# A two-block transformer forward pass: the opening of block 1 with four parts' modulation columns on TensorE, rotation tables made earlier, and more buffers for whole weights

## The chip, the cores and the metric

The kernel runs on one core of a Trainium2 chip. One launch computes everything. The metric is device microseconds of that launch; before the change it is 1609.81 us, the median of three runs (1606.74 to 1617.44).

The engines are named as the profile names them: PE is TensorE (PEld is its weight loading), DVE is VectorE, ACT is ScalarE, POOL is GpSimd, SP is the engine whose queue issues the loads.

## What is computed

256 tokens of 1024 features pass through two transformer blocks. Block 1 has block attention, a recurrent mixer (RWKV7) and an expert layer; block 2 has two attentions and a gated layer. What matters here is how block 1 begins:

```python
def first_block(x, c, positions, w_ada, b_ada, norm1_g, w_in, ...):
    mod = (jax.nn.silu(c) @ w_ada[l] + b_ada[l])[:, None, :]
    sh1, sc1, gt1, sh2, sc2, gt2 = jnp.split(mod, 6, axis=-1)
    xn = rms_norm(h, norm1_g[l]) * (1.0 + sc1) + sh1
    proj = xn @ w_in[l]
    qm, km, vm, zrw, gate_logits = jnp.split(proj, split_at, axis=-1)
    qm = rope_partial(rms_norm(qm ...), positions)
    ...
    zrw = token_shift(zrw, rwkv_mu[l])
    zr, zk, zv, zw, za, zg = jnp.split(zrw, rwkv_split, axis=-1)
    ...
```

`c` is one vector of 1024 numbers, so `mod` is a vector; `sh1` and `sc1` are its first 2048 entries (shift and scale). `rms_norm` divides each token by the root of the mean of its squares. `rope_partial` multiplies by the sine and cosine of positions times frequencies.

## The kernel before, in words

**Layout.** Activations stand transposed, 128 features on the partitions and 256 tokens along the free axis, in eight chunks. All weights come from HBM as units of 128 x 1024 float32 (512 KB), loaded by SP's queue in an order that is written out. Most matmuls are made of three passes: a weight unit `raw` is split by ACT into `hi` (line 304, a rounded copy) and by DVE into `lo = raw - hi` (line 306), the activations are split likewise into `xh` and `xl`, and PE sums `xh` by `hi`, `xl` by `hi` and `xh` by `lo`.

**The opening.** `block1_mixer` opens with the first norm, its modulation and the first products, woven together over eight parts `d` of 128 features. Ahead of the loop, eight `sq` tiles (`x` squared, line 660) are summed over the partitions by matmuls with a matrix of ones into `ss` (line 661). The loop of line 705 then runs `n` from 0 to 9 and calls three functions, each one step behind the last:

- `open_ada(n)` loads two units `aw` of `w_ada` (line 668). Each holds four 128 x 256 blocks; the 256 columns are 128 of shift and 128 of scale for part `n`. DVE multiplies each block with a column of `silu(c)`, held in the tile `sil`, and adds it up in `aacc`, 128 x 256: one pass on line 672 and seven on line 674. For every second part it also loads a unit `whole` (line 678), and for each part a unit that is split into `hi` and `lo`.
- `open_norm(n - 1)` sums `aacc` over the partitions by two matmuls with one column of ones (line 687), which gives shift and scale as two 128 x 1 columns in PSUM. DVE adds `b_ada` (line 689, `mod`) and makes the gain column `gs` (line 431). `norm_chunk` then makes the normalized tile: `nt` on DVE (line 437, `x` times gain times `rs`, the inverse root that `norm_stat` made of `ss` on lines 368 and 369), `xh` on ACT (438), `x` on ACT (440, the unsplit tile), `xl` on DVE (441).
- `open_mm(n - 2)` multiplies part `n - 2` into six PSUM tiles `z` of 128 x 512: eight matmuls of `xh` by `hi`, four of `x` by `whole` in float32 (line 703), eight of `xl` by `hi`, eight of `xh` by `lo` (line 699).

At `n == 1`, ahead of the three calls, stand `rope_tables` (the load of `pos`, eleven DVE passes, and sine and cosine on ACT, lines 592 to 611), the load of ACT's table for logarithm and exponential (it shows at line 708), and `norm_stat`. Sine needs another ACT table, which is loaded at line 607.

**What sets the order.** A scheduling layer puts the instructions in a fixed order for each engine; an engine works through its own list and waits by semaphores for the others. Pools of buffers set when a load may be issued: `aw` has 5 buffers, `whole` 2, `aacc` 3, `x` 3, `hi` and `lo` 4 each in the opening, `raw` 4, and the small PSUM tiles `mmo` 2.

After the opening, the same `z` tiles are shifted by one token and the rest of both blocks follows.

Of the kernel before, what the change touches and what calls it, by code (L numbers as in the profile page):

```python
# [6 lines left out]
F32 = mybir.dt.float32  # L7
# [9 lines left out]
T = 256  # L17
# [15 lines left out]
W3 = 1  # L33
NS = 2
AHEAD = 1
DECAY = float(np.exp(-0.5))

AT_B1, AT_U, AT_V, AT_B2, AT_FF = 192, 192, 192, 192, 192
# [231 lines left out]
class Prog:  # L270
# [360 lines left out]
    def block1_mixer(self):  # L631
        tc, v, s, pe, sy = self.tc, self.v, self.s, self.pe, self.sy
        wu, bp, mm = self.wu, self.bp, self.pe.matmul
# [9 lines left out]
        def shift(ps, mi, dst):  # L643
            s.activation(dst, ps, AF.Copy, scale=omm[:, mi:mi + 1])
            v.scalar_tensor_tensor(dst[:, 1:], ps[:, :T - 1], self.col("mu", mi), dst[:, 1:], OP.mult, OP.add)


        with ExitStack() as st:
            E = st.enter_context
            sp = E(tc.tile_pool(name="open", bufs=1, side="right", reuse_waits="tile"))  # L650
            zp = E(tc.tile_pool(name="zps", bufs=1, space=PSUM, reuse_waits="tile"))
            h = sp.tile([128, 8, T], F32, name="x0")
            for q in range(2):
                sy.dma_start(h[:, 4 * q:4 * q + 4], self.a["xT"][:, 4 * q:4 * q + 4])
            zps = [zp.tile([128, 2, T], F32, name=f"z{j}") for j in range(6)]
            slabs, whole, xs = [], [], {}
            ss = self.mm.tile([128, T], F32, name="mmo", tag="mm")
            for d in range(8):
                sq = sp.tile([128, T], F32, name="sq", tag="sq", bufs=6)
                s.activation(sq, h[:, d], AF.Square)  # L660
                mm(ss, self.ones, sq, start=(d == 0), stop=(d == 7))
            accs = {}

            def open_ada(d):
                accs[d] = acc = sp.tile([128, T], F32, name="aacc", tag="aacc", bufs=3)
                for i in range(2):
                    w = sp.tile([128, 4, T], F32, name="aw", tag="aw", bufs=5)
                    sy.dma_start(w, self.a["w"][wu["ada0"] + 2 * d + i].rearrange("p (k n) -> p k n", k=4))
                    for k in range(4):
                        sc = self.silu["c"][:, 4 * i + k:4 * i + k + 1]  # L670
                        if i + k == 0:
                            v.tensor_scalar(acc, w[:, k], sc, None, OP.mult)
                        else:
                            v.scalar_tensor_tensor(acc, w[:, k], sc, acc, OP.mult, OP.add)
                u = wu["rw"] + d // 2 * 3
                if d % 2 == 0:
                    whole.append(sp.tile([128, 1024], F32, name="whole", tag="whole", bufs=2))
                    sy.dma_start(whole[-1], self.a["w"][u])
                slabs.append(self.wsplit(u + 1 + d % 2, pool=sp, bufs=4, lead=0))
                if d == 3:  # L680
                    sy.dma_start(self.c0, self.a["w"][wu["c0"]])

            def open_norm(d):
                acc = accs.pop(d)
                pm = self.mm.tile([128, 2], F32, name="mmo", tag="mm")
                for i in range(2):
                    mm(pm[:, i:i + 1], acc[:, i * 128:(i + 1) * 128], self.ones[:, 0:1], start=(i == 0), stop=(i == 1), skip_group_check=True)
                for i in range(2):
                    v.tensor_tensor(self.mod1[:, 8 * i + d:8 * i + d + 1], pm[:, i:i + 1], self.col("b1", 8 * i + d), OP.add)
                gs = self.norm_gain("n1", self.mod1[:, 8 + d:9 + d], 1, d)  # L690
                xs[d] = sp.tile([128, T], F32, name="x", tag="x", bufs=3)
                self.norm_chunk(h[:, d], gs, self.mod1[:, d:d + 1], xh[:, d], xl[:, d], xs[d])

            def open_mm(d):
                hi, lo = slabs[d]
                C = lambda i: slice(i * 128, (i + 1) * 128)
                for part, (lhs, rhs) in enumerate(((hi, xh), (hi, xl), (lo, xh))):
                    for j in range(4, 12):
                        mm(zps[j // 2][:, j % 2], lhs[:, C(j - 4)], rhs[:, d], start=(d + part == 0 and j % 2 == 0),
                           stop=(d == 7 and part == 2), skip_group_check=True)  # L700
                    if part == 0:
                        for j in range(4):
                            mm(zps[j // 2][:, j % 2], whole[d // 2][:, C(d % 2 * 4 + j)], xs[d], start=(d + j % 2 == 0), stop=(d == 7), skip_group_check=True)

            for n in range(10):
                if n == 1:
                    self.rope_tables()
                    tc.keep_in_program_order(s.preload_act_table_set(LN_EXP))
                    self.norm_stat(ss)
                for f, d in ((open_ada, n), (open_norm, n - 1), (open_mm, n - 2)):  # L710
                    if 0 <= d < 8:
                        f(d)
            zs = []

            def shift_z(c):
                for i in range(3):
                    z = e4("z")
                    j = 3 * c + i
                    shift(zps[j // 2][:, j % 2], (4, 0, 8)[i] + c, z)
                    zs.append(z)  # L720

            zwa, sg = bp.tile([128, T], F32, name="zwa"), bp.tile([128, T], F32, name="sg")
            thw = bp.tile([128, T], F32, name="thw")
            v.memset(thw[64:128], 0.0)
            shift_z(0)
            shift(self.t_unit(wu["rwl"], xh, xl), 12, zwa)
            t0 = self.sm.tile([128, T], F32, name="t0", tag="nt", bufs=2)
            s.activation(t0[0:64], zwa[0:64], AF.Exp, scale=-2.0)
            v.tensor_scalar(t0[0:64], t0[0:64], 2.0 ** 60, None, OP.min)
            s.activation(t0[0:64], t0[0:64], AF.Ln, bias=1.0)  # L730
            s.activation(t0[0:64], t0[0:64], AF.Exp, scale=-1.0)
            v.tensor_scalar(thw[0:64], t0[0:64], 2.0, -1.0, OP.mult, OP.add)
            v.memset(zwa[0:64], 0.0)
            shift_z(1)
            shift(self.t_unit(wu["rwl"] + 1, xh, xl), 13, sg)
            t0 = self.sm.tile([128, T], F32, name="t0", tag="nt", bufs=2)
            self.sigmoid(sg, sg, t0)
            shift_z(2)
            shift_z(3)
# [25 lines left out]
        def rwkv_pair(c):  # L765
# [6 lines left out]
            self.sigmoid(ld, ps, t0, nw0[:, c:c + 1])  # L772
            s.activation(ld, ld, AF.Copy, scale=-DECAY)
            L = e1("L")
# [234 lines left out]
        def fill():  # L1009
            yield from self.tn_steps(wu["mv"], 4, xh, xl, [vm[:, 0], vm[:, 1]], pp, "gm")  # L1010
            yield from staggered([moba_pair(c) for c in range(4)], 3)
            for j in range(16):
                ps = self.t_unit(wu["gate"] + j, xh, xl)
                t0 = e1("t0", "eg", 2)
                gt = e4("gt")
                self.sigmoid(gt, ps, t0)
                self.gates.append(gt)
                yield
            for j in range(4):
                for i, ps in enumerate(self.t_units(*self.wsplit(wu["pmr"] + 2 * j), 4, 2, mh, ml, 1024, [(pp, "gm")])):  # L1020
                    g = self.gates[4 * j + 2 * i]
                    v.tensor_tensor(g, ps, g, OP.mult)
                yield

        f, n, tick = fill(), 0.0, 0
# [41 lines left out]
    def peer(self):  # L1067
# [230 lines left out]
        while i < 128:  # L1298
            for _ in u_pair(i):
                n += 1  # L1300
                new = []
                while prog["c"] < T and prog["c"] // 4 * (left - AHEAD) <= n * (T // 4):
                    new.append(choose(gp))
# [484 lines left out]
```

## Time and profile before

| | before |
|---|---|
| median of three runs | 1609.81 us (1606.74 to 1617.44) |
| the profiled execution | 1610.28 us |
| its span in the trace | 1608.0 us, 33360 instructions |
| PE busy | 1562.9 us (97%) |
| PEld busy | 1504.4 us (94%) |
| DVE busy | 1263.5 us (79%) |
| ACT busy | 1019.4 us (63%) |
| the opening, up to its last `z` matmul | 69.94 us |
| DMA, mean over the span | 189 GB/s |

The trace is of one execution. An engine's busy time counts its own instructions alone; what an engine waited for is inferred from semaphores. "Idle before" is the time in which the engine had nothing to do ahead of that instruction, with what ended it. PEclk is the share of full clock that TensorE was granted: 1.00 is 2.4 GHz, 0.50 is 1.2 GHz. In the timeline, instructions of one line that follow each other are one row with a count; a row's time includes the latency of its last instruction, so a row may overlap the next of its engine. A float32 matmul leaves two records, the others leave one.

### The profile page before, as it was taken

The numbers are of one execution on the slowest core, as the hardware profiler recorded it, in microseconds if no ns is written. First come the engines' busy times: TensorE is split into PE (matmuls) and PEld (weight loads), VectorE is DVE, ScalarE is ACT, GpSimd is POOL, SyncE is SP. The second block draws the span as 40 slices with busy tenths as digits, with TensorE's granted clock in tenths as the row PEclk, the third lists the DMA queues.
The fourth block names the chain that finished last, engine by engine and source line by source line (L and its number), as shares of the span: only waits on it lengthen the run. The fifth ranks groups of instructions, "written<-read, shape, count | busy, mean of one in ns | idle before, by whom it ended". The sixth has DMA issues, their size and how long they took to land.

```text
span 1608.0 us, 33360 instructions
## 1 busy us (share of the span) xinstructions
PE 1562.9 (97%) x13022; PEld 1504.4 (94%) x13022; DVE 1263.5 (79%) x2731; ACT 1019.4 (63%) x2093; POOL 6.5 (0%) x43
## 2 busy tenths in 40 slices
PE   5999999999999999999999999999999999999998
PEld 5888898989999999999999999999888998989998
DVE  7887887878789777888877777777798986777776
ACT  4475765555545799998654445444679786665553
POOL 0000000000000000000000000000000000000000
PEclk8999999999999999999999999999999999999999
DMA  8632336645544544444688878788666322435553
GB/s 308 247 106 93 119 128 225 231 141 179 183 166 170 184 161 169 169 159 171 212 275 274 274 261 278 269 287 271 203 211 224 133 87 102 168 121 186 190 189 105
DMA packets 85261, 306.63 MB, mean 191 GB/s; under 512 B 9456, under 2 KB 10992, under 8 KB 84976
## 3 DMA queue, kind: packets, MB, share of 16 engines
q1 hardware_dynamic: 85104, 304.51, 55.4%
q8 instruction: 102, 1.67, 0.4%
q14 instruction: 55, 0.45, 0.1%
HBM read 303.42 MB, written 1.05 MB: 189 GB/s over the span
## 4 chain that ended last, share of the span: by engine, by line
PE 85%; DVE 8%; ACT 3%; DMA 2%; issue 1%; SPq 0%; DVEq 0%; ACTq 0%
PE mmo L322 14%; PE mmo L325 14%; PE mmo L323 14%; PE acc L322 7%; PE acc L323 7%; PE acc L325 7%; DVE lo L306 3%; DMA raw<-w 2%; PE pg L1263 2%; PE facc L322 1%; PE facc L325 1%; PE facc L323 1%; ACT hi L304 1%; PE pxt L893 1%; PE pz L881 1%
## 5 line engine op out<-in xcount | busy, mean ns | idle before, releaser
L304 ACT ACTIVATE hi<-raw 128x1024 fp32r<-128x1024 f32 (+1 forms) x465 | 490.4, 1057 | 370.0 <-PE mmo L323 136.1
L306 DVE TENSOR_TENSOR lo<-raw,hi 128x1024 fp32r<-128x1024 f32 (+1 forms) x465 | 565.2, 1218 | 165.7 <-ACT hi L304 162.6
L322 PE MATMUL mmo<-xh,hi 128*128 128x256 f32 x2032 | 498.8, 286 | 1.6 <-ACT hi L304 0.6
L323 PE MATMUL mmo<-xl,hi 128*128 128x256 f32 x2032 | 490.4, 281 | 0.0
L322 PEld LDWEIGHTS mmo<-xh,hi 128*128 128x128 f32 x2032 | 382.8, 189 | 5.7 <-ACT hi L304 2.1
L323 PEld LDWEIGHTS mmo<-xl,hi 128*128 128x128 f32 x2032 | 383.3, 189 | 1.9 <-issue 0.2
L325 PE MATMUL mmo<-xh,lo 128*128 128x256 f32 x2032 | 283.3, 281 | 4.7 <-DVE lo L306 4.6
L325 PEld LDWEIGHTS mmo<-xh,lo 128*128 128x128 f32 x2032 | 255.6, 189 | 7.2 <-DVE lo L306 6.5
L322 PE MATMUL acc<-Hh,hi 128*128 128x256 f32 x1024 | 241.8, 278 | 0.5 <-ACT Hh L363 0.5
L323 PE MATMUL acc<-Hl,hi 128*128 128x256 f32 x1024 | 241.0, 278 | 0.0
L322 PEld LDWEIGHTS acc<-Hh,hi 128*128 128x128 f32 x1024 | 192.3, 188 | 0.7 <-ACT Hh L363 0.7
L323 PEld LDWEIGHTS acc<-Hl,hi 128*128 128x128 f32 x1024 | 192.5, 188 | 0.1
L325 PE MATMUL acc<-Hh,lo 128*128 128x256 f32 x1024 | 139.4, 277 | 0.0
L325 PEld LDWEIGHTS acc<-Hh,lo 128*128 128x128 f32 x1024 | 127.3, 188 | 0.0
L388 DVE SCALAR_TENSOR_TENSOR acc<-raw,sil,acc 128x1024 f32<-128x1024 f32 x70 | 89.8, 1283 | 44.8 <-DMA raw<-w 44.7
L1245 ACT ACTIVATE D<-iota,i 128x128 f16<-128x128 f16 x256 | 84.6, 404 | 0.2
L1252 DVE TENSOR_TENSOR B<-O,iT 128x512 f16<-128x512 f16 x128 | 46.1, 417 | 0.0
L323 PE MATMUL facc<-Hl,hi 128*128 128x256 f32 x176 | 42.8, 281 | 0.0
L322 PE MATMUL facc<-Hh,hi 128*128 128x256 f32 x176 | 42.8, 281 | 0.0
L364 DVE TENSOR_TENSOR Hl<-hidA,Hh 128x256 fp32r<-128x256 f32 x96 | 40.0, 418 | 0.0
L363 ACT ACTIVATE Hh<-hidA 128x256 fp32r<-128x256 f32 x96 | 38.2, 400 | 0.0
L1246 ACT ACTIVATE A<-D 128x512 f16<-128x512 f16 x64 | 37.8, 628 | 0.0
(503 smaller groups left out, 2273.3 us busy)
## 6 DMA issues: line engine op xcount, KB each, us to landing
raw<-w SPq DMA_DIRECT2D x542, 512.0 KB, 4.1
aw<-w SPq DMA_DIRECT2D x16, 512.0 KB, 7.3
raw<-w SPq DMA_DIRECT2D x6, 384.0 KB, 3.3
whole<-w SPq DMA_DIRECT2D x4, 512.0 KB, 7.2
c<-w SPq DMA_DIRECT2D x3, 512.0 KB, 6.2
x<-xT SPq DMA_DIRECT2D x2, 512.0 KB, 5.7
hres<-xT SPq DMA_DIRECT2D x1, 1024.0 KB, 5.5
sk<-w SPq DMA_DIRECT2D x2, 512.0 KB, 5.6
```

The lines of the kernel that those rows point to most:

```text
L304: self.s.activation(hi[:, :n], r[:, :n], AF.Copy)
L306: self.v.tensor_tensor(lo[:, :n], r[:, :n], hi[:, :n].bitcast(F32), OP.subtract)
L322: m(out, whi[w], xhi[x], start=start, stop=False, skip_group_check=True)
L323: m(out, whi[w], xlo[x], start=False, stop=False, skip_group_check=True)
L325: m(out, wlo[w], xhi[x], start=False, stop=stop, skip_group_check=True)
L363: self.s.activation(hi, src, AF.Copy)
L364: self.v.tensor_tensor(lo, src, hi.bitcast(F32), OP.subtract)
L388: v.scalar_tensor_tensor(acc, w, sc, acc, OP.mult, OP.add)
L1245: s.activation(D[:, j], iota, AF.Abs, bias=i1[:, t0 + j:t0 + j + 1])
L1246: s.activation(A, D, AF.Relu, scale=-1.0, bias=1.0)
L1252: v.tensor_tensor(B[p], O, row(1 + p), OP.mult)
L1263: mm(pg[:, j], B[p][:, :, j], A[:, j], start=(j + p == 0), stop=(j == 3 and p == 1), skip_group_check=True)
```

## The change

Three edits, all in the opening.

1. For the parts `d < PEADA = 4`, `open_ada` makes no DVE passes. Instead, PE takes each 128 x 128 half of an `aw` block as its weights and the column of `silu(c)` as its one moving column: 2 units x 4 blocks x 2 halves are 16 float32 matmuls of one column for each part, 64 in all. They add up shift and scale in the small PSUM tile at once, so that for these parts `open_norm` needs no sums by ones and no `aacc`. Parts 4 to 7 are as before.
2. `rope_tables`, ACT's table loads and `norm_stat` stand at `n == 0` in place of `n == 1`, that is ahead of the first part's modulation.
3. `whole` has four buffers in place of two, and `sq` four in place of six.

```diff
--- before.py
+++ after.py
@@ -33,6 +33,7 @@
 W3 = 1
 NS = 2
 AHEAD = 1
+PEADA = 4
 DECAY = float(np.exp(-0.5))
 
 AT_B1, AT_U, AT_V, AT_B2, AT_FF = 192, 192, 192, 192, 192
@@ -656,25 +657,33 @@
             slabs, whole, xs = [], [], {}
             ss = self.mm.tile([128, T], F32, name="mmo", tag="mm")
             for d in range(8):
-                sq = sp.tile([128, T], F32, name="sq", tag="sq", bufs=6)
+                sq = sp.tile([128, T], F32, name="sq", tag="sq", bufs=4)
                 s.activation(sq, h[:, d], AF.Square)
                 mm(ss, self.ones, sq, start=(d == 0), stop=(d == 7))
             accs = {}
 
             def open_ada(d):
-                accs[d] = acc = sp.tile([128, T], F32, name="aacc", tag="aacc", bufs=3)
+
+                if d < PEADA:
+                    accs[d] = self.mm.tile([128, 2], F32, name="mmo", tag="mm")
+                else:
+                    accs[d] = acc = sp.tile([128, T], F32, name="aacc", tag="aacc", bufs=3)
                 for i in range(2):
                     w = sp.tile([128, 4, T], F32, name="aw", tag="aw", bufs=5)
                     sy.dma_start(w, self.a["w"][wu["ada0"] + 2 * d + i].rearrange("p (k n) -> p k n", k=4))
                     for k in range(4):
                         sc = self.silu["c"][:, 4 * i + k:4 * i + k + 1]
-                        if i + k == 0:
+                        if d < PEADA:
+                            for r in range(2):
+                                mm(accs[d][:, r:r + 1], w[:, k, r * 128:(r + 1) * 128], sc, start=(i + k + r == 0),
+                                   stop=(i == 1 and k == 3 and r == 1), skip_group_check=True)
+                        elif i + k == 0:
                             v.tensor_scalar(acc, w[:, k], sc, None, OP.mult)
                         else:
                             v.scalar_tensor_tensor(acc, w[:, k], sc, acc, OP.mult, OP.add)
                 u = wu["rw"] + d // 2 * 3
                 if d % 2 == 0:
-                    whole.append(sp.tile([128, 1024], F32, name="whole", tag="whole", bufs=2))
+                    whole.append(sp.tile([128, 1024], F32, name="whole", tag="whole", bufs=4))
                     sy.dma_start(whole[-1], self.a["w"][u])
                 slabs.append(self.wsplit(u + 1 + d % 2, pool=sp, bufs=4, lead=0))
                 if d == 3:
@@ -682,8 +691,8 @@
 
             def open_norm(d):
                 acc = accs.pop(d)
-                pm = self.mm.tile([128, 2], F32, name="mmo", tag="mm")
-                for i in range(2):
+                pm = acc if d < PEADA else self.mm.tile([128, 2], F32, name="mmo", tag="mm")
+                for i in range(2) if d >= PEADA else ():
                     mm(pm[:, i:i + 1], acc[:, i * 128:(i + 1) * 128], self.ones[:, 0:1], start=(i == 0), stop=(i == 1), skip_group_check=True)
                 for i in range(2):
                     v.tensor_tensor(self.mod1[:, 8 * i + d:8 * i + d + 1], pm[:, i:i + 1], self.col("b1", 8 * i + d), OP.add)
@@ -703,7 +712,7 @@
                             mm(zps[j // 2][:, j % 2], whole[d // 2][:, C(d % 2 * 4 + j)], xs[d], start=(d + j % 2 == 0), stop=(d == 7), skip_group_check=True)
 
             for n in range(10):
-                if n == 1:
+                if n == 0:
                     self.rope_tables()
                     tc.keep_in_program_order(s.preload_act_table_set(LN_EXP))
                     self.norm_stat(ss)
```

The change moves instructions on three engines. On PE, right behind the squares, before (a row is a line of the kernel, the operation, out<-in, the shape written, and how many follow each other; `z_118` to `z_123` are the six PSUM tiles):

```order
L661 MATMUL mmo<-sq,ones 128x256 x8
L687 MATMUL mmo<-ones,aacc 128x1 x2
L699 MATMUL z_120<-xh,hi 128x256 x2
L699 MATMUL z_121<-xh,hi 128x256 x2
L699 MATMUL z_122<-xh,hi 128x256 x2
L699 MATMUL z_123<-xh,hi 128x256 x2
L703 MATMUL z_118<-x,whole 128x256
L687 MATMUL mmo<-ones,aacc 128x1 x2
L703 MATMUL z_118<-x,whole 128x256
L703 MATMUL z_119<-x,whole 128x256 x2
L699 MATMUL z_120<-xl,hi 128x256 x2
```

and of the changed kernel at the same place:

```order
L662 MATMUL mmo<-sq,ones 128x256 x8
L678 MATMUL mmo<-sil,aw 128x1 x32
L708 MATMUL z_120<-xh,hi 128x256 x2
L708 MATMUL z_121<-xh,hi 128x256 x2
L708 MATMUL z_122<-xh,hi 128x256 x2
L708 MATMUL z_123<-xh,hi 128x256 x2
L712 MATMUL z_118<-x,whole 128x256 x2
L712 MATMUL z_119<-x,whole 128x256 x2
L678 MATMUL mmo<-sil,aw 128x1 x8
L708 MATMUL z_120<-xl,hi 128x256 x2
```

The one-column matmuls of parts 0 and 1 stand ahead of all of `z`, and the first eight of part 2 inside part 0's `z`; its other eight come further down in the same part, behind two `xh,lo` matmuls. Part 3's first eight come at the same place of part 1's `z`, its last eight behind seven of part 2's eight `xh,hi` matmuls.

On DVE, from the adds of part 3 to the `nt` of part 4, before:

```order
L689 TENSOR_TENSOR mod_85<-mmo,cols 128x1 x2
L674 SCALAR_TENSOR_TENSOR aacc<-aw,sil,aacc 128x256
L431 SCALAR_TENSOR_TENSOR gs<-mod_85,cols 128x1
L674 SCALAR_TENSOR_TENSOR aacc<-aw,sil,aacc 128x256
L437 SCALAR_TENSOR_TENSOR nt<-x_115,gs,rs 128x256
L674 SCALAR_TENSOR_TENSOR aacc<-aw,sil,aacc 128x256 x2
L441 SCALAR_TENSOR_TENSOR xl<-nt,mod_85,xh 128x256
L674 SCALAR_TENSOR_TENSOR aacc<-aw,sil,aacc 128x256 x2
L689 TENSOR_TENSOR mod_85<-mmo,cols 128x1 x2
L431 SCALAR_TENSOR_TENSOR gs<-mod_85,cols 128x1
L437 SCALAR_TENSOR_TENSOR nt<-x_115,gs,rs 128x256
```

and of the changed kernel between the same two places:

```order
L698 TENSOR_TENSOR mod_85<-mmo,cols 128x1 x2
L432 SCALAR_TENSOR_TENSOR gs<-mod_85,cols 128x1
L438 SCALAR_TENSOR_TENSOR nt<-x_115,gs,rs 128x256
L442 SCALAR_TENSOR_TENSOR xl<-nt,mod_85,xh 128x256
L307 TENSOR_TENSOR lo<-raw,hi 128x1024
L681 TENSOR_SCALAR aacc<-aw,sil 128x256
L683 SCALAR_TENSOR_TENSOR aacc<-aw,sil,aacc 128x256 x7
L698 TENSOR_TENSOR mod_85<-mmo,cols 128x1 x2
L432 SCALAR_TENSOR_TENSOR gs<-mod_85,cols 128x1
L438 SCALAR_TENSOR_TENSOR nt<-x_115,gs,rs 128x256
```

Part 4's passes stood between the instructions of part 3's norm (its first two even ahead of the adds); now all eight stand behind that norm and a `lo`. From part 4's `nt` on the order on DVE is that of before.

On ACT, between the squares and the first `xh`, before:

```order
L660 ACTIVATE sq<-x_115 128x256 x8
L368 ACTIVATE rs<-mmo,eps 128x256
L369 ACTIVATE rs<-rs 128x256
L304 ACTIVATE hi<-raw 128x1024
L607 ACT_TABLE_LOAD
L607 ACTIVATE sin_171<-ang 128x256
L611 ACTIVATE cos_170<-kr 128x256
L708 ACT_TABLE_LOAD
L304 ACTIVATE hi<-raw 128x1024
L438 ACTIVATE xh<-nt,mod_85 128x256
```

and of the changed kernel:

```order
L661 ACTIVATE sq<-x_115 128x256 x8
L608 ACT_TABLE_LOAD
L608 ACTIVATE sin_150<-ang 128x256
L612 ACTIVATE cos_149<-kr 128x256
L717 ACT_TABLE_LOAD
L369 ACTIVATE rs<-mmo,eps 128x256
L305 ACTIVATE hi<-raw 128x1024
L370 ACTIVATE rs<-rs 128x256
L439 ACTIVATE xh<-nt,mod_85 128x256
```

The two table loads, sine and cosine moved ahead of `rs`, and the `hi` of part 1 is now behind the first `xh`. On SP's queue the load of `pos` moved ahead of the first two `aw` and the first `whole`, where it stood behind them; the rest of that queue is as before. Behind the opening all engines have the same order as before.

## Rows read from the trace of the kernel before

**Rows 1.** The page, part 1: busy us of each engine, share of span, instructions.

```profile
PE 1562.9 (97%) x13022; PEld 1504.4 (94%) x13022; DVE 1263.5 (79%) x2731; ACT 1019.4 (63%) x2093; POOL 6.5 (0%) x43
```

**Rows 2.** Busy time by stretch (us from the start), the opening; columns in the first line.

```profile
core 0: us, PE busy (x) PEld busy (x) DVE busy (x) ACT busy (x) POOL busy (x), PEclk, DMA share, GB/s
...
12.00:17.20 5.20, 0.65 (x5) 0.52 (x4) 4.43 (x15) 3.23 (x4) 0.00 (x0) 1.00 1.03 414
17.20:22.50 5.30, 0.00 (x0) 0.00 (x0) 5.19 (x13) 3.56 (x6) 0.00 (x0) 0.50 0.97 393
22.50:27.40 4.90, 4.84 (x17) 4.41 (x18) 4.59 (x13) 0.41 (x2) 0.00 (x0) 0.50 0.99 365
27.40:42.20 14.80, 14.80 (x109) 14.12 (x108) 13.34 (x37) 5.57 (x9) 0.00 (x0) 1.00 0.70 255
```

**Rows 3.** Timeline: start us, us, engine line operation tiles xcount [idle before, releaser]; the opening.

```profile
6.34 5.70 PE L661 MATMUL mmo<-sq,ones 128*128 128x256 f32 x16 [6.34 <-ACT sq L660]
...
8.48 1.33 ACT L660 ACTIVATE sq<-x 128x256 f32<-128x256 f32 x4 [1.27 <-DMA x<-xT]
...
9.81 0.35 DVE L672 TENSOR_SCALAR aacc<-aw,sil 128x256 f32<-128x256 f32 x1 [5.33 <-DMA aw<-w]
...
13.86 0.61 PE L687 MATMUL mmo<-ones,aacc 128*128 128x1 f32 x4 [1.81 <-DVE aacc L674]
...
14.56 1.06 ACT L304 ACTIVATE hi<-raw 128x1024 fp32r<-128x1024 f32 x1 [1.55 <-DMA raw<-w]
...
15.64 1.28 ACT L607 ACT_TABLE_LOAD   x1
...
17.39 0.42 ACT L607 ACTIVATE sin<-ang 128x256 f32<-128x256 f32 x1 [0.47 <-DVE ang L606]
...
22.56 2.08 PE L699 MATMUL z<-xh,hi 128*128 128x256 f32 x8 [8.09 <-ACT xh L438]
...
29.81 0.53 PEld L687 LDWEIGHTS mmo<-ones,aacc 128*128 128x128 f32 x4
```

**Rows 4.** Chain that ended last, in order of time: start us, us, what; part 7.

```profile
65.43 0.94 PE z L699 x8
66.38 1.73 PE z L703 x8
68.11 1.83 PE z L699 x16
```

**Rows 5.** Groups by line, 0 to 70 us: xcount | busy us, mean ns | idle before.

```profile
L674 DVE SCALAR_TENSOR_TENSOR aacc<-aw,sil,aacc 128x256 f32<-128x256 f32 x56 | 27.0, 482 | 1.1
...
L687 PE MATMUL mmo<-ones,aacc 128*128 128x1 f32 x32 | 4.6, 249 | 1.8 <-DVE aacc L674 1.8
```

**Rows 6.** Waits, 0 to 75 us (SP's queue: to 60): us, times, longest us.

```profile
PE z L699 <- ACT xh L438: 10.3, 3, 8.1
...
SPq L678 <- PE z L703: 10.3, 2, 6.0
```

**Rows 7.** Timeline again, parts 3 and 4 of the opening.

```profile
33.23 0.33 SPq L678 DMA_DIRECT2D whole<-w  x1
...
35.93 0.35 DVE L672 TENSOR_SCALAR aacc<-aw,sil 128x256 f32<-128x256 f32 x1
...
41.20 0.50 PE L687 MATMUL mmo<-ones,aacc 128*128 128x1 f32 x4
...
42.20 0.48 DVE L437 SCALAR_TENSOR_TENSOR nt<-x,gs,rs 128x256 f32<-128x256 f32 x1
42.60 1.22 DVE L306 TENSOR_TENSOR lo<-raw,hi 128x1024 fp32r<-128x1024 f32 x1
42.72 0.51 ACT L438 ACTIVATE xh<-nt,mod 128x256 fp32r<-128x256 f32 x1 [2.02 <-DVE nt L437]
...
43.73 0.35 DVE L672 TENSOR_SCALAR aacc<-aw,sil 128x256 f32<-128x256 f32 x1
...
45.77 1.89 PE L703 MATMUL z<-x,whole 128*128 128x256 f32 x8
```

## The prediction

> **What bounds the kernel now.** I read the page first, then the busy time by stretch, the timeline of the opening, the chain of waits, the groups by line and the waits. The page says that TensorE (PE) is busy for 1562.9 us, 97% of the span [rows 1]. By stretch, this is not so at the start: from 12 to 22.5 us PE works 0.65 us of 10.5, and the clock granted to it falls from full to half (2.4 to 1.2 GHz) at 17.2 us and is back only at 27.4 us, 4.9 us after matmuls have begun to run again [rows 2]. The change touches nothing behind 70 us; that is 1538 of the 1608 us. All that can be gained or lost lies ahead of it, and most of the room is in the 10 us in which PE stands still.
>
> What PE waits for there is a chain [rows 3]. VectorE waits for the first `aw` until 9.81 us and makes part 0's eight passes; PE, which waited for them, sums them over the partitions at 13.86 us. Then the rotation tables, two activation table loads and a `hi`/`lo` pair stand in front of the first normalized tile, and `z` starts at 22.56 us, after 8.1 us of waiting for `xh`. Behind that, one part costs PE 0.94 + 1.73 + 1.83 = 4.50 us at full clock [rows 4]. Until 42 us PE and VectorE are about equally loaded (14.80 and 13.34 us of 14.80, [rows 2]); later VectorE leads, and the opening's `z` ends at 68.11 + 1.83 = 69.94 us [rows 4]. Of all its waits for `xh` in the opening (10.3 us in 3, [rows 6]) PE spends 8.1 us on the first.
>
> **What is removed.** 32 passes: 28 at 482 ns [rows 5] and 4 at 350 ns [rows 3], 14.9 us of VectorE's own time, and eight one-column sums of PE. Before 42 us this is nearly half of what VectorE does.
>
> **What is added.** 64 one-column matmuls on PE. A float32 matmul leaves two records (32 for the 16 `L687` matmuls, [rows 5]), so these are 128 records, each with a full load of 128 columns of weights. Their price isn't `L687`'s mean of 249 ns, which holds one record's latency. Four of its weight loads in a row take 0.53 us [rows 3], 0.13 us each with the latency of the last in it, and `z`'s 16 records with a weight load each take 1.83 us, 0.114 us each [rows 4]. I take 0.112 us: 128 x 0.112 = 14.3 us. The bound above, at full clock, is 0.13 us (+2.3 us). For the bound below the trace has nothing, since nothing in it runs more densely; rival C takes half. At half clock it is about twice as much (eight `z` records in 2.08 us at 22.56 [rows 3], in 0.94 us at 65.43 [rows 4]). So 14.9 us leave VectorE and 14.3 us come to PE, which has 10 us of idle time ahead of 22.5 us and next to none between there and 42.
>
> The Trainium skill (page "TensorE: Matmul & The Clock Gate", section "Back-to-back issue gap") gives an isolated matmul of 1 to 64 columns a floor of about 25 ns. By that the columns would cost an estimated 3.2 us, not 14.3; the 0.114 us between records that each load weights speaks against it here, and the sum goes by the row.
>
> **The sum at full clock.** PE is through with the squares at 6.34 + 5.70 = 12.04 us [rows 3]. Part 0's 32 records end at 15.6 us. Part 1's wait for VectorE's two adds of part 0, whose PSUM buffer they take over (0.3 us), and end at 19.5 us. Then `z` of part 0 starts, 3.1 us sooner than now. In the new order part 2's 32 records stand inside part 0's `z`: 19.5 + 4.5 + 3.6 = 27.6 us. Part 3's first 16 stand inside part 1's `z`, the last 16 behind seven of the eight `xh,hi` matmuls of part 2: 27.6 + 4.5 + 1.8 + 0.8 + 1.8 = 36.5 us.
>
> What follows is serial, because part 4's eight passes stand in VectorE's queue behind part 3's `nt`, `xl` and a `lo`, where before they were strewn in between. From the columns' end: two adds, `gs` and `nt` until `xh` starts 1.1 us (41.20 + 0.50 to 42.72, [rows 7]), `xh` 0.5, `hi` 1.06 [rows 3], `lo` until the next pass 1.13 (42.60 to 43.73, [rows 7]): the passes begin at 40.3 us, where they began at 35.93, and are done at 44.3 (4.0 from 9.81 to 13.86, [rows 3]). PE's own queue gives nearly the same: what is left of part 2 (3.7) and part 3 (4.5) ends at 44.7 us, and part 4's two sums stand behind it. From the sums to `nt` it is 41.20 to 42.20: part 4's `nt` at about 45.8 instead of 42.20, **3.6 us later**. From there on VectorE's order is that of before, with the same 27.7 us to the end of the opening.
>
> **The clock.** Between 12 and 22.5 us four one-column records did not keep it up [rows 2, 3]; no row shows what a dense stream of them does. The bounds: it holds (0 us), or the stream is worth no more to the clock than the idle time that it replaces. I take the second, since with one moving column each these records are nearer to the `L687` ones ahead of the fall than to `z`'s. Then the clock falls at 17.2 us as before: the 2.4 us of part 1 that are left double, and `z` starts at about 22.0 us. Half clock lasts 4.9 us into `z` as before, which costs 2.45 us. Together 4.85 us.
>
> **Edits costed at nothing.** Four `whole` buffers: SP waits for these buffers now (10.3 us in 2 waits, [rows 6]), but the third `whole`, issued at 33.23 us, is first read at 45.77 us [rows 7]. The cover is VectorE's path to part 4; without it, up to the 6.0 us of the longest wait. Four `sq` buffers: PE's squares run without a gap from 6.34 to 12.04 us while ACT is done at 9.81 [rows 3]; at most one square, 0.4 us. Tables ahead: ACT now loads two tables (2 x 1.28) and makes sin and cos (2 x 0.42) behind the squares, until 13.2 us; then half of `rs`, the `hi` of the `raw` that lands at 14.5, the rest of `rs` until 16.0 (0.4 us), VectorE's `lo` until 16.8; `xh` of part 0 is there at 17.8 us. The cover is PE's columns until 19.5 us; with quicker columns the 1.7 us of slack are gone, and PE waits for `xh` instead. On SP's queue the 128 KB of `pos` now pass the first two `aw` and the first `whole`, and delay each by 0.3 us at 414 GB/s [rows 2], by 1.3 if they take as long as 512 KB: `aw` at 9.8 us may slip to 11, and PE has squares until 12.04.
>
> Sum for the likeliest: +3.6 + 4.85 = +8.4 us on the profiled execution's 1610.28, so 1618.7; on the median of 1609.81, 0.5 us lower, 1618.2. I say **1618.5 us**.
>
> **The rivals.** (A) The clock holds through the columns: only the 3.6 us stay, 1613.9 us. For it: PE is busy nearly without a pause from 6.3 us on. Against it: the four records of [rows 3]. 0.27. The Trainium skill (same page, "Part 1: The HAM clock gate") lets the clock follow how busy TensorE has lately been; by that a dense stream holds it, and the time is A's. The rows agree that it falls after idling; none shows this stream.
>
> (B) The forecast. 0.50.
>
> (C) The columns run faster than 0.112 us. From 0.112 - 3.6 / 128 = 0.084 us on, the 3.6 us are repaid. At 0.056 us parts 2 and 3 save 3.6 us and the first two 1.7 at most (then `xh` is late), so -1.7: 1608.6 us, or 1611 if the pause before `xh` drops the clock and costs 2.45. Against it: no denser run of weight loads in any row. 0.15.
>
> (D) The other side, slower by over 1%: half clock lasts through all the columns, since those inside `z` thin it out. 17.2 to 36.5 us double, +19.3 + 3.6: 1633.2 us. It decides from 12.5 us lost, that is 25 us at half clock after 17.2. Against it: `z` brought the clock back in 4.9 us [rows 2]. 0.05. The other 0.03 are collisions of loads that I don't see.
>
> **How the numbers follow.** The low end is C's 1608.5. The high end is B with half clock also through part 2's columns (+3.6 us): 1622.3, rounded to 1623. D and the tails of C and B are left out. About 1%, 16 us, is what a measurement of this kernel can tell from no change; A, B and C all lie within it. Faster by over 1% would need more than PE's whole pause: 0.01. Slower: D and a little, 0.06. Same: 0.93.
>
> **What would show it.** VectorE's busy time ahead of 42 us falls by over 10 us; one-column records stay 0.11 us apart at full clock (C: less). `z` starts at 22.0 us, with half clock from 17.2 to about 27 (A: 19.5, full clock). Part 4's passes begin at 45 us (A: 40.3), its `nt` at 50.6 (A: 45.8), and the opening ends at 78.4 us instead of 69.94 (A: 73.5). The third `whole` is issued earlier, and nobody starts earlier for it. The 1538 us behind the opening stay. I am wrong if part 4's passes begin before 36 us, or if the rest moves by more than 2 us.

## The result, and the profile after

The changed kernel takes 1619.97 us, the median of 20 runs (1613.34 to 1628.88), against 1609.53 us of the kernel before (20 runs, 1603.39 to 1617.44). The ratio is 1.0063, with a 95% interval of 1.0046 to 1.0080: 10 us slower, 7 to 13. The forecast was 1618.5 us in a range of 1608.5 to 1623.0. One run of wide0134 below (2211.26 us) and one of the kernel before (3965.84 us) lie far from all others and are left out of the ratios.

The profiled execution is one of the long ones, 1627.65 us with a span of 1625.3. Its busy time, part 1 of the page (before: [rows 1]):

```profile
PE 1585.3 (98%) x13134; PEld 1526.1 (94%) x13134; DVE 1252.3 (77%) x2699; ACT 1019.5 (63%) x2093; POOL 6.5 (0%) x43
```

VectorE lost 11.2 us net, PE gained 22.4, and there are 112 more PE records: 128 for the columns, less 16 for the sums by ones. The busy time of the opening by stretch (us, then busy us and count of each engine, granted clock of TensorE, share of the DMA engines, GB/s), cut where the clock changes; [rows 2] have the like of before:

```profile
core 0: us, PE busy (x) PEld busy (x) DVE busy (x) ACT busy (x) POOL busy (x), PEclk, DMA share, GB/s
12.00:17.40 5.40, 5.08 (x46) 5.00 (x45) 2.44 (x8) 3.84 (x6) 0.00 (x0) 1.00 1.03 421
17.40:27.70 10.30, 10.30 (x43) 9.58 (x42) 3.54 (x9) 2.76 (x5) 0.00 (x0) 0.50 1.00 406
27.70:31.10 3.40, 3.40 (x32) 3.40 (x32) 0.00 (x0) 0.00 (x0) 0.00 (x0) 1.00 0.41 118
31.10:37.90 6.80, 6.80 (x28) 6.35 (x28) 2.58 (x6) 1.85 (x3) 0.00 (x0) 0.50 0.67 267
37.90:61.80 23.90, 20.94 (x156) 19.90 (x154) 14.24 (x35) 4.67 (x7) 0.00 (x0) 1.00 0.54 201
61.80:68.60 6.80, 5.41 (x19) 4.88 (x20) 3.53 (x10) 1.85 (x3) 0.00 (x0) 0.50 0.40 148
68.60:84.10 15.50, 14.89 (x110) 14.12 (x110) 11.57 (x26) 6.31 (x11) 0.95 (x4) 1.00 0.62 228
```

The pause of PE from 12 to 22.5 us is gone, as the change meant: PE is busy from 12 to 37.9 us but for 0.32 us, in which part 1's columns wait for VectorE's adds of part 0 (between the first two rows of the next fence). But it has half clock in three stretches, 23.9 us in all, where before there was one of 10.2. The clock falls at 17.4 us, with PE busy since 15.95 us (busy as the profile counts it: a matmul of one column keeps PE busy too). The chain of waits shows what PE did there (start us, us, what, records):

```profile
12.17 3.48 PE mmo L678 x32
...
15.95 5.67 PE mmo L678 x32
21.61 1.92 PE z L708 x8
...
26.94 2.08 PE mmo L678 x16
...
30.28 2.37 PE mmo L678 x16
...
39.79 1.68 PE mmo L678 x16
```

`L678` are the one-column matmuls: 3.48 / 32 = 0.109 us per record at full clock, 1.68 / 16 = 0.105 further down. Part 1's records, the second row, run into the fall and take 5.67 us. The timeline of VectorE and PE shows how late the rest is (before: [rows 7], 35.93 and 42.20 us):

```profile
48.43 0.35 DVE L681 TENSOR_SCALAR aacc<-aw,sil 128x256 f32<-128x256 f32 x1
...
53.96 0.49 DVE L438 SCALAR_TENSOR_TENSOR nt<-x,gs,rs 128x256 f32<-128x256 f32 x1
...
82.93 1.11 PE L708 MATMUL z<-xh,lo 128*128 128x256 f32 x8
```

Part 4's passes begin at 48.43 and its `nt` at 53.96 us, 11.8 us later than before; the opening ends at 84.04 us, 14.1 us later. Behind it lie 1625.3 - 84.0 = 1541.3 us, where it was 1538.1. The waits name who sat idle (us in total, times, longest):

```profile
ACT xh L439 <- DVE nt L438: 47.2, 8, 10.3
DVE mod L698 <- PE mmo L678: 21.0, 4, 8.1
...
PE z L708 <- ACT xh L439: 5.0, 3, 2.8
```

Now VectorE waits 21 us for PE's columns. Before, it waited for PE only for the sums by ones, 2.6 us in 5 times.

### The profile page after: what moved, and what is told of

Read it like the earlier page. It is cut to its first block, busy times and chain, and to the rows that moved or that the text cites. A ratio compares the mean times of both kernels' runs of the same rounds, so it can differ in the third digit from the quotient of the medians.

```text
span 1625.3 us, 33548 instructions
## 1 busy us (share of the span) xinstructions
PE 1585.3 (98%) x13134; PEld 1526.1 (94%) x13134; DVE 1252.3 (77%) x2699; ACT 1019.5 (63%) x2093; POOL 6.5 (0%) x43
## 4 chain that ended last, share of the span: by engine, by line
PE 85%; DVE 7%; DMA 3%; ACT 3%; issue 1%; DVEq 0%; SPq 0%; ACTq 0%
PE mmo L323 14%; PE mmo L324 14%; PE mmo L326 14%; PE acc L323 6%; PE acc L324 6%; PE acc L326 6%; DMA raw<-w 3%; DVE lo L307 3%; PE pg L1272 2%; PE z L708 1%; PE facc L326 1%; PE facc L324 1%; PE facc L323 1%; PE pxt L902 1%; PE pz L890 1%; ACT hi L305 1%
```

## Experiments

Three theories were set against each other. CLOCK: the one-column matmuls cost what their weight loads cost, and besides they don't hold TensorE's clock, which falls ahead of and inside the first parts of `z`. LOADS: the 64 weight-loading matmuls alone make the time, and the clock is beside the point. ROPE: the tables moved ahead of the first norm cost the time.

In this table, the end of the opening is that of the last `z` matmul in the profiled execution, "half clock" lists the stretches in it from 12 us up to there, and the ratio is to the kernel before, with its 95% interval. The experiments were run in two sets, each with runs of the kernel before beside it (medians 1609.51 and 1610.83 us), so a ratio isn't the quotient of two medians of the table.

| kernel | end of opening, us | half clock, us | median, us | ratio |
|---|---|---|---|---|
| before | 69.94 | 17.2 to 27.4 | 1609.5 | |
| changed, first trace | 84.04 | 17.4 to 27.7, 31.1 to 37.9, 61.8 to 68.6 | 1619.97 | 1.0063 (1.0046 to 1.0080) |
| changed, second trace | 78.97 | 15.9 to 26.1, 60.3 to 63.7 | 1622.41 | 1.0076 (1.0046 to 1.0106) |
| mix | 73.00 | 54.2 to 57.6 | 1613.16 | 1.0019 (0.9995 to 1.0042) |
| mixb | 70.93 | 17.7 to 24.5 | 1614.58 | 1.0029 (1.0005 to 1.0052) |
| wide4 | 66.85 | none | 1611.81 | 1.0000 (0.9978 to 1.0022) |
| wide0134 | 64.47 | none | 1607.01 | 0.9974 (0.9954 to 0.9994) |
| narrow2 | 78.01 | 16.9 to 27.2, 40.8 to 47.6, 57.9 to 61.3 | 1619.50 | 1.0056 (1.0033 to 1.0080) |
| rope_only | 69.50 | 15.4 to 25.6 | 1608.18 | 0.9999 (0.9975 to 1.0022) |
| cols_only | 85.78 | 15.8 to 39.7, 63.5 to 70.4 | 1631.25 | 1.0133 (1.0101 to 1.0164) |

What lies behind the opening (span less its end) took 1533 to 1546 us in these executions: longest in the two whose opening ends first, 1545.9 in wide4 and 1545.6 in wide0134, shortest in the one whose opening ends last, 1533.4 in cols_only. Whether an early end of the opening lengthens the rest, one trace of each can't show. So the end of the opening is read from the trace, and the times only with their intervals.

Each run also carries its mean granted clock over the whole span, and these means agree with the traces: 0.9914 in the 20 runs of the changed kernel, 0.9869 in cols_only, 0.9897 in narrow2, 0.9927 in mixb, 0.9932 in rope_only, 0.9962 in mix and in wide0134, 0.9972 in wide4; the kernel before has 0.9943 and 0.9931 in the two sets, where PE stood still in part of the time at half clock. From the changed kernel to mix it is 0.0048 of the span, an estimated 7.8 us, where the medians are 6.8 us apart.

### mix: 128 moving columns for parts 0 and 1

```diff
+            srep = sp.tile([128, 8, 128], F32, name="srep")
+            for k in range(8):
+                v.tensor_scalar(srep[:, k], self.ones, self.silu["c"][:, k:k + 1], None, OP.mult)
...
+                    W = 128 if d < 2 else 1
-                    accs[d] = self.mm.tile([128, 2], F32, name="mmo", tag="mm")
+                    accs[d] = self.mm.tile([128, 2 * W], F32, name="mmo", tag="mm")
...
-                                mm(accs[d][:, r:r + 1], w[:, k, r * 128:(r + 1) * 128], sc, ...
+                                mm(accs[d][:, r * W:(r + 1) * W], w[:, k, r * 128:(r + 1) * 128],
+                                   srep[:, 4 * i + k] if d < 2 else sc, ...
...
-                    whole.append(sp.tile([128, 1024], F32, name="whole", tag="whole", bufs=4))
+                    whole.append(sp.tile([128, 1024], F32, name="whole", tag="whole", bufs=3))
```

> The changed kernel, but the moving operand of parts 0 and 1 is silu(c) repeated over 128 columns (made by eight DVE passes of 128x128), parts 2 and 3 keep one column; three `whole` buffers for room. The order on DVE is that of the changed kernel, on PE nearly. Theory CLOCK (one-column matmuls don't hold TensorE's clock; the first half-clock stretch costs some 5 us): full clock through 17 to 28 us, part 0's z starts at about 19.4 us in place of 21.5, the opening ends at 71 to 74 us, time +1 to +4 us on before: 1611 to 1614. Theory LOADS (64 more weight-loading matmuls cost what they cost, the clock would have fallen anyway): no nearer to before than the changed kernel, +8 to +12 us, z of part 0 at 21 us or later.

Measured: `z` starts at 18.8 us, the opening ends at 73.00, 1613.16 us. The stretches of mix, ahead of `z`, of part 0's `z`, and later (columns as above, here and in all such fences below):

```profile
12.00:18.70 6.70, 6.70 (x60) 6.57 (x60) 3.00 (x9) 4.40 (x8) 0.00 (x0) 1.00 1.03 420
18.70:27.00 8.30, 8.30 (x68) 8.09 (x68) 3.92 (x12) 2.92 (x7) 0.00 (x0) 1.00 1.03 418
27.00:54.20 27.20, 24.21 (x179) 22.89 (x178) 18.14 (x42) 7.38 (x12) 0.00 (x0) 1.00 0.79 297
54.20:57.60 3.40, 3.40 (x12) 2.87 (x11) 1.10 (x4) 0.17 (x1) 0.00 (x0) 0.50 0.08 27
```

CLOCK holds, LOADS falls: as many weights are loaded as in the changed kernel, on nearly the same order of VectorE, and with more columns behind those of the first two parts the clock stays at full from 12 to 54 us. Parts 2 and 3 still have one column each here, and the clock didn't fall while they stood among `z` matmuls. The late short stretch comes behind a wait of PE for `xh`.

Mix differs from the changed kernel in two more things. Its columns of parts 2 and 3 stand a little earlier on PE, and PE doesn't pause between the columns of parts 0 and 1. That the pause of 0.32 us, rather than the single columns, brought the clock down isn't borne out: the second fall in the changed kernel's first trace, at 31.1 us, came with PE busy ever since 15.95 us, and in the kernel before PE waited 1.40 us for `xh` ahead of 51.43 us and the clock stayed up.

### wide4: 128 columns for all four parts

The edit is that of mix with `W = 128` and `srep` for all parts `d < 4`. (The eight passes that make `srep` take 1.7 us of VectorE, ahead of the first weights.)

> As the changed kernel, but with silu(c) repeated over 128 columns for all four parts. The scheduler orders it a little differently: part 4's passes on DVE still stand behind part 3's norm, but all 32 columns of part 2 and half of part 3's stand earlier. CLOCK: full clock from 10.6 us to the end of the opening, which ends at 66 to 68 us, time 2 to 4 us below before: 1606 to 1608. LOADS: at least the 3.6 us of the columns at full clock above before, 1613 to 1620.

Measured: no half clock from 12 us to the end of the opening at 66.85 us, 3.1 us ahead of before. The ratio is 1.0000, 0.9978 to 1.0022. The opening came out as CLOCK said, the time did not: 1611.8 us where 1606 to 1608 were expected. The traced execution is the longest of its 12 (1614.99 us), and it took 1545.9 us behind the opening, more than any other trace; 3 us out of 1610 are within the interval. From 31.3 us on its opening reads

```profile
31.30:66.90 35.60, 35.51 (x254) 33.49 (x253) 27.52 (x67) 11.93 (x20) 0.90 (x4) 1.00 0.74 281
```

and its chain has the price of the wide matmuls:

```profile
12.75 7.14 PE mmo L681 x64
...
21.25 3.57 PE mmo L681 x32
```

3.57 / 32 = 0.112 us per record with 128 columns, against 0.105 to 0.109 with one: the 127 others cost 0.003 to 0.007 us each time.

### mixb: 128 columns for parts 2 and 3 only

The edit is that of mix with `srep` for parts 2 and 3 and one column for parts 0 and 1.

> The other half of mix: parts 0 and 1 with one moving column, parts 2 and 3 with silu(c) over 128 columns. CLOCK: the first half-clock stretch is there (17 to 27 us), the second is not; z of part 0 at 21.5 us, opening ends at 69 to 72 us (some 3.5 us behind wide4's 66.9), 1609 to 1615 us. LOADS: as the changed kernel or as wide4, with no step between them.

Measured: the first fall alone, and shorter than in the changed kernel (17.7 to 24.5 us):

```profile
17.70:24.50 6.80, 6.80 (x31) 6.62 (x31) 2.51 (x9) 2.67 (x5) 0.00 (x0) 0.50 1.03 419
24.50:71.00 46.50, 46.15 (x347) 44.21 (x346) 32.11 (x75) 14.73 (x25) 0.92 (x4) 1.00 0.76 278
```

The opening ends at 70.93 us, 4.1 us behind wide4. The 6.80 us at half clock, in which PE was busy throughout, make 3.4 of these; in the rest the waits and the order on PE differ a little too. The time, 1614.58 us, is in the expected band.

### The changed kernel, traced again

> The changed kernel once more, for a second trace of it. CLOCK: the first half-clock stretch (17 to 27 us) is there again, since it follows from the columns ahead of z; the second (31 to 38 us in the first trace) and the third (62 to 69 us) depend on how the half-used stretches of PE fall, and may be missing. With the first alone the opening ends at 76 to 79 us, with all three at 84. Median 1617 to 1622 us. LOADS: the opening's end doesn't follow the half-clock stretches.

Measured: 1622.41 us, ratio 1.0076, just above the expected median. The trace has the first stretch and only a short one late:

```profile
15.90:26.10 10.20, 10.20 (x42) 9.57 (x43) 4.55 (x9) 2.90 (x6) 0.00 (x0) 0.50 1.03 418
26.10:60.30 34.20, 29.86 (x227) 28.66 (x226) 19.33 (x47) 8.27 (x13) 0.00 (x0) 1.00 0.66 250
60.30:63.70 3.40, 3.40 (x12) 2.84 (x11) 1.18 (x5) 0.11 (x1) 0.00 (x0) 0.50 0.06 22
```

and its timeline

```profile
21.18 2.06 PE L708 MATMUL z<-xh,hi 128*128 128x256 f32 x8
...
44.35 0.35 DVE L681 TENSOR_SCALAR aacc<-aw,sil 128x256 f32<-128x256 f32 x1
...
49.88 0.48 DVE L438 SCALAR_TENSOR_TENSOR nt<-x,gs,rs 128x256 f32<-128x256 f32 x1
...
77.87 1.10 PE L708 MATMUL z<-xh,lo 128*128 128x256 f32 x8
```

puts the end of the opening at 78.97 us, 9.0 us behind before. The same program, with the same order on each engine, ended its opening at 84.04 us in the first trace, where the clock fell a second time at 31.1 us, among part 0's `z` and part 2's columns. Whether that second stretch comes is a matter of the execution; why it comes in one and not in the other isn't shown. LOADS gives no reason for such a difference.

### rope_only: the other edits without the columns

```diff
-PEADA = 4
+PEADA = 0
```

> Only the other edits: no part's columns on PE (PEADA = 0), rotation tables, table loads and norm_stat ahead of part 0, four whole and four sq buffers. CLOCK: these edits are worth nothing or little, since DVE bounds the opening as before: z of part 0 at 18 to 21 us, opening ends at 69 to 71 us, 1608 to 1611. Rival ROPE (the tables ahead of the first norm delay it and cost the time): 1614 to 1620.

Measured: `z` starts at 20.13 us in place of 22.56, and the opening ends at 69.50 us in place of 69.94; the ratio is 0.9999, 0.9975 to 1.0022. ROPE falls. The 2.4 us won at the start are nearly gone at the end: VectorE still has all its passes, and PE waits for it later, longest here:

```profile
51.11 1.19 PE L708 MATMUL z<-xh,hi 128*128 128x256 f32 x8 [2.19 <-ACT xh L439]
```

This covers all three edits that I had costed at nothing (tables, `whole`, `sq`) together, without the columns; they weren't run one by one.

### cols_only: the columns without the other edits

```diff
-                if n == 0:
+                if n == 1:
                     self.rope_tables()
...
-name="whole", tag="whole", bufs=4
+name="whole", tag="whole", bufs=2
...
-name="sq", tag="sq", bufs=4
+name="sq", tag="sq", bufs=6
```

> Only the columns: four parts' one-column matmuls on PE; rotation tables stay at n == 1, two whole and six sq buffers as before. CLOCK and LOADS: slower than before by 6 to 15 us, since z of part 0 then also waits for the tables (23 us): 1616 to 1625, opening ends at 76 to 86 us. ROPE: as before, within 3 us of 1609.5.

Measured: 1631.25 us, ratio 1.0133: 21 us over before, where I had expected 6 to 15. The profiled execution, with 1621.6 us the shortest of its runs, already ends the opening at 85.78 us. Its first stretch at half clock and the chain in it:

```profile
15.80:39.70 23.90, 23.90 (x104) 23.17 (x105) 9.92 (x24) 7.36 (x12) 0.00 (x0) 0.50 0.55 221
```

```profile
15.54 6.75 PE mmo L678 x32
...
24.93 3.20 PE mmo L678 x16
...
31.76 3.21 PE mmo L678 x16
```

PE is busy in all of the 23.9 us, at half clock in all of them, through the columns of parts 1 and 2 and the whole of part 0's `z`. A record takes 0.20 to 0.21 us there. This comes near to what the prediction called rival D, in a neighbour of the changed kernel; only part 3's columns came later, at full clock. The other edits, worth nothing by themselves, spare the columns 9 to 11 us of this (1631.25 against 1622.41 and 1619.97); which of the three does it isn't shown.

### narrow2: one column, for parts 0 and 1 only

```diff
-PEADA = 4
+PEADA = 2
```

> The changed kernel with PEADA = 2: one-column matmuls for parts 0 and 1 alone. CLOCK: the first stretch at half clock stays, the columns inside z are gone, and with them the second; DVE gets its first passes at 22 to 26 us in place of 48; opening ends at 72 to 76 us, 1612 to 1616 us. LOADS: half of the changed kernel's +10 us, 1615.

Measured: 1619.50 us, opening 78.01 us. I missed this one: half of the columns give nearly all of the loss. The columns inside `z` are gone, but two stretches at half clock have come, behind waits of PE for `xh` and for part 3's `aacc`:

```profile
40.80:47.60 6.80, 5.93 (x20) 5.22 (x21) 3.88 (x9) 1.85 (x3) 0.00 (x0) 0.50 0.70 254
47.60:57.90 10.30, 7.50 (x54) 6.83 (x53) 9.31 (x24) 2.36 (x5) 0.00 (x0) 1.00 0.63 227
57.90:61.30 3.40, 3.34 (x12) 3.07 (x13) 2.14 (x5) 1.35 (x3) 0.00 (x0) 0.50 0.39 158
```

PE works 7.50 of 10.30 us between them. In the kernel before it had 14.80 us of work in 14.80 from 27.4 us on [rows 2]; as I read it, because its long first pause had put it behind VectorE. The time isn't proportional to the number of columns, which speaks against LOADS too.

### wide0134: 128 columns, for parts 0, 1, 3 and 4

The edit is wide4 with `d < PEADA` replaced by `d in (0, 1, 3, 4)`.

> As wide4, but the parts whose columns PE makes are 0, 1, 3 and 4, so that DVE has part 2's passes to make while PE does the others. CLOCK with the order of DVE: full clock through the opening, part 2's passes before 24 us, and the opening ends at 64 to 66 us, 4 to 6 us ahead of before: 1604 to 1607 us. If the order of DVE is worth nothing: as wide4, 66.9 us and 1609 to 1612.

Measured: 1607.01 us, ratio 0.9974, 0.9954 to 0.9994: faster than the kernel before by 4 us (1 to 7), and so than the changed one. The opening ends at 64.47 us. Part 2's passes begin on VectorE at 21.20 us, and PE has no gap and full clock:

```profile
18.80:35.50 16.70, 16.70 (x135) 16.28 (x135) 11.16 (x27) 5.96 (x10) 0.00 (x0) 1.00 1.03 418
35.50:64.50 29.00, 29.00 (x210) 27.64 (x209) 23.30 (x54) 10.89 (x18) 0.88 (x4) 1.00 0.74 285
```

From 12 us on PE is now the bound of the opening. Against wide4 the opening ends 2.4 us sooner, in one trace of each; the intervals of the two ratios overlap, so the times alone don't tell them apart.

## Why the prediction was right, and where its steps were off

**Direction and size.** 10.4 us between the medians against 8.7 forecast (1618.5 less 1609.81), by the mechanism named as the likeliest. The clock fell at 17.4 and 15.9 us in the two traces while PE made nothing but one-column matmuls, and mix shows that it stays up when the same loads have 128 columns behind them. Rival A is out for this kernel: a busy PE didn't hold the clock. By the rule of the Trainium skill that was weighed there (page "TensorE: Matmul & The Clock Gate", "Part 1: The HAM clock gate"), a PE that is busy keeps its clock; here PE was busy for 10.30 of 10.30 us at half clock.

**The price of a record** was taken as 0.112 us; it is 0.109 and 0.105 at full clock, 0.20 to 0.21 at half. Rival C, which needed 0.084, is out. The Trainium skill's floor of about 25 ns for an isolated matmul (same page, "Back-to-back issue gap") was not approached by these records, which each load 128 columns of weights.

**The first stretch** was to cost 4.85 us: `z` at 22.0 us and half clock until 27. It was 21.18 and 26.1 us in the second trace, 21.48 and 27.7 in the first. In mixb, where it is 6.80 us long, it makes 3.4 us of the 4.1 to wide4.

**The serial term** was to cost 3.6 us at full clock. In the second trace part 4's `nt` comes 7.7 us later than before. The 10.20 us at half clock make an estimated 5.1 of these, which leaves 2.6. The last column ends at 40.7 us, 35.6 without those 5.1, where the sum had 36.5; from there to `nt` it took 9.2 us, 9.3 in the sum. So the chain behind the columns was right, and the sum had the columns' end 0.9 us too late. In mix, which has full clock there, `nt` comes at 43.83 us, only 1.6 us later than before: PE began its columns 0.4 us sooner, didn't pause for the adds (0.3), and part 3's last eight stand 11 matmuls further ahead (an estimated 1.3).

**What was missing** is the tail. "From there on the same 27.7 us" held in neither trace: 49.88 to 78.97 is 29.1 us in the second and 53.96 to 84.04 is 30.1 in the first. From the `nt` of one part to that of the next, all of the growth lies between parts 5 and 6: 6.01 us before, 7.47 in the second trace and 8.44 in the first; the steps from 4 to 5 and from 6 to 7 are 8.16 and 7.29 us in all three. PE now has done its earlier parts and waits 2.8 us for part 5's `xh`; the clock falls, part 5's matmuls run at half clock, and part 6's two sums stand in PE's order behind fourteen of their records. VectorE waits for these sums before it can make part 6's `nt`, here in the kernel before and in the second trace (3.17 us in the first):

```profile
54.32 0.22 DVE L689 TENSOR_TENSOR mod<-mmo,cols 128x1 f32<-128x1 f32 x2 [0.73 <-PE mmo L687]
63.45 0.23 DVE L698 TENSOR_TENSOR mod<-mmo,cols 128x1 f32<-128x1 f32 x2 [2.18 <-PE mmo L696]
```

In the second trace the errors cancel: `nt` 7.7 us late instead of 8.4, the tail 1.4 us longer. That its opening ended within 0.6 us of the forecast 78.4 is luck to that extent.

**Rival D** is not as far off as its 0.05 said. The first trace has 23.9 us at half clock in three stretches, near the 25 us from which D decides, and its run is 1.1% over the median of before; cols_only came near to D. That the clock falls again inside `z` was given as the high end of the range (1622.3 us). It fell in one of the two traces, and 7 of the 20 runs of the changed kernel lie above 1625 us, while the others reach up to 1623.7. That the upper ones are those with a second fall is argued from the one trace among them, 1627.65 us, and it can't be all: the mean granted clock of the seven is 0.9904, of the thirteen others 0.9920, an estimated 2.6 us of time, where their mean times are 9.3 us apart. Of the 9.5 us between the spans of the two traces, 5.1 lie in the opening and 4.4 behind it. Where the rest comes from stays open.

**Edits at nothing**: without the columns, rope_only confirms it for the three together; beside the columns they aren't idle, since without them the time is 9 to 11 us longer (cols_only). The third `whole` is issued at 29.44 us instead of 33.23 and serves nobody, as foreseen. VectorE's busy time between 12 and 42.2 us fell from 27.6 to 8.6 us, by 19 where over 10 was forecast; part 4's passes too went behind 48 us.

**The rest of the kernel** was to stay within 2 us. It was 1541.3 and 1536.8 us in the two traces, 1538.1 before; but the traces of all ten executions range from 1533 to 1546. By its own sign (2 us) the first trace would count against the prediction; one trace couldn't have shown it either way.

## What to carry to other kernels

Work that is moved from a loaded engine to an idle TensorE has to be judged by what it does to the clock as well: here a stream of matmuls with one moving column kept PE busy, and still the clock fell to half, and the matmuls behind it took twice as long. Where a product with a vector is put on TensorE, look whether the same weights can be used with more columns; here 128 equal columns cost 0.112 us per record in place of 0.105 to 0.109, and with them the loss of 10 us was gone (wide4, ratio 1.0000). Spread over parts 0, 1, 3 and 4, so that VectorE had part 2's passes to make from 21.20 us on, the same work gained 4 us over before. And when work leaves an engine, look at the order of what it still has: in the changed kernel VectorE's remaining passes stood behind the very results that it now had to wait for.

## What the runs showed that I had not expected

- The same program has openings of 84.04 and 78.97 us in two executions, by stretches of half clock that come in one and not in the other. The changed kernel's runs spread from 1613 to 1629 us, 16 us, where the kernel before has 14.
- The clock also fell late in the opening, behind gaps in which PE waited for `xh`: in both traces of the changed kernel, in mix, narrow2 and cols_only, each with a gap of 2.77 us (narrow2 also behind gaps of 0.85 and 1.71 us). In the three executions in which PE had next to no gap there (mixb, wide4, wide0134: 46.15 us of work in 46.50 in mixb) it stayed up, and so it did behind 2.19 us in rope_only and 1.40 us in the kernel before.
- A pause of PE can be of use: the 10 us in which it stood still in the kernel before let it follow VectorE later with few waits. With the pause filled, the waits come later, where they cost clock too (narrow2). This is read from the traces, not tried by itself.
